# The FFN's opening in a two-layer diffusion backbone: the first token quarter split earlier, four blocks' first products ahead of the sums, the sums' halves laid out by need

## The chip, the cores and the metric

The kernel runs on one core of a Trainium2 chip. The metric is the device time of one execution in microseconds (us); the time of a kernel is the median of its runs. Engines are named as the profile names them: PE (TensorE), PEld (its weight loads), DVE (VectorE), ACT (ScalarE), POOL (GpSimd), SP (SyncE, which only issues DMAs here).

## What is computed

Two layers of a backbone over 512 latent tokens and 256 context tokens of width 1024. Each layer has a mixing sub-layer (three scan mixers side by side and one output projection) and a SwiGLU feed-forward network (FFN) with 2816 hidden channels. Layer 0 computes both token groups through the FFN (768 tokens), layer 1 only the latent ones (512 tokens). What matters here is the end of the mixing sub-layer and the FFN:

```python
mixed_l = jnp.concatenate([gla_l, ssd_l, ret_l], axis=-1) @ w_out[l]
lat = lat + gt1 * rms_norm(mixed_l, norm_mix_post[l])
h_l = modulate(rms_norm(lat, norm_ffn_pre[l]), sh2, sc2)
lat = lat + gt2 * rms_norm(swiglu(h_l, ffn_w13[l], ffn_w2[l]), norm_ffn_post[l])

def swiglu(h, w13, w2):
    gate, up = jnp.split(h @ w13, 2, axis=-1)
    return (jax.nn.silu(gate) * up) @ w2
```

## The kernel before

**Numbers in halves.** Every large matmul is done on pairs: a value x is stored as hi (x cast to a narrower format, by ACT) and lo (x minus hi, by DVE or POOL), and each product is three matmuls, hi·hi, hi·lo and lo·hi. `split` (line 366) does it for a weight tile (`whi` on line 368, `wlo` on line 369), `rsplit` (line 1261) for activations.

**The FFN's first matmul as a 2x2 scheme with seven products.** The activations `whole` (written by `pre_norm` in the output projection stage, one block of 128 tokens after another) are cut into four quarters: b11 and b21 are the lower and upper 512 channels of the first half of the tokens, b12 and b22 those of the second half. For each of 22 blocks of 128 hidden channels (`ffn_up(f)`), the two weight columns are cut into a11, a12, a21, a22, and seven products are taken: a11·b11, a12·b21, s2·t2, s3·t3, s1·t1, a22·t4, s4·b22, where t1 to t4 are sums and differences of the quarters of the activations and s1 to s4 those of the weights. A product (`prod`, its matmuls on line 1289) is 12 matmuls of 384 columns in layer 0 and of 256 columns in layer 1. The weights' sums are made in `load13`: two on POOL (lines 417, 418), two on DVE (lines 419, 420), after the raw weights have landed (DMA on line 405), and are then split. The raw tiles stand in two places that alternate by block: even blocks in pool `wp`, odd blocks in pool `F`.

**The opening.** a11·b11 and a12·b21 need no sums, so for the first NA blocks (3 in layer 0, 4 in layer 1) they are taken ahead (`up_first`, `up_gate`, lines 1295 to 1305), with a weight unit of their own (`w13a`, which holds only a11 and a12). `ffn_up` of these blocks then does the other five products. Before that, per 128 tokens of the first half: the split of b11 (lo on DVE) and of b21 (lo on POOL), the sums t1, t2, t4 (DVE, lines 1275, 1276, 1278) and t3 (POOL, line 1277), the splits of t1 to t4 (lo on DVE) and of b22 (lo on POOL). All four sums' hi halves share one 24 KB buffer of pool `hp`, all lo halves the other; that other buffer is the one that holds `whole`, so no lo half of a sum can be written before the last reader of `whole` is done.

**The stage ahead of it.** The output projection runs over 6 blocks of tokens in layer 0 and 4 in layer 1 (`out_front`, `out_back`): transposes, 96 matmuls of a block (line 497), then for the block before it the norm after the projection (`post_norm`), the residual and the norm ahead of the FFN (`pre_norm`: transposes on line 306, scale and shift into `whole` on lines 312 and 314). Between these, PE also takes the matmuls of the adaptive norm's modulation (`Ada.some`: 48 steps in layer 0 and 32 in layer 1, four matmuls each on lines 203 and 206, with a 512 KB weight load `araw` in a ring of three buffers). Most steps stand ahead of the output stage in the program, the last ten of layer 0 and the last two of layer 1 behind it.

**What sets the order.** The program is written in order; a planner places each instruction on its engine's queue by that order and its own estimate of times, and each engine then works its queue strictly in order. Pools of SBUF are stacks that lie on each other's ground: the pools of the opening, `F`, `FB` and `HR`, are opened when the output stage's pools and the modulation's pool `adp` are closed, and take their place.

Of the kernel before, what the change touches and what calls it, by code (L numbers as in the profile page):

```python
# [11 lines left out]
F32 = mybir.dt.float32  # L12
# [70 lines left out]
def tile_backbone(ctx: ExitStack, tc: tile.TileContext, a: dict, out: bass.AP, dbg=None):  # L83
# [364 lines left out]
    for l in range(NL):  # L448
# [23 lines left out]
        NA = 3 if l + 1 < NL else 4  # L472
# [94 lines left out]
    for l in range(NL):  # L567
# [587 lines left out]
        ada.some(len(ada.todo) - 12)  # L1155
# [9 lines left out]
        whole = pt(hp, "H", [128, 8, tot])  # L1165

# [59 lines left out]
        ada.some(len(ada.todo))  # L1226
        rx.close()
        mx.close()
        ax.close()


        hn = tot // 2
        npos = tot // 128
        n2 = npos // 2
# [13 lines left out]
        fx = ctx.enter_context(ExitStack())  # L1248
        HR = fx.enter_context(pool(f"HR{l}", side="right"))
        FB = fx.enter_context(pool(f"FB{l}", side="right"))  # L1250
        with pool(f"F{l}") as F:
            state["F"] = F
            bhi = pt(FB, "bhi", [128, 3, 4, hn], F32R, bufs=1)
            blo = pt(FB, "blo", [128, 3, 4, hn], F32R, bufs=1)
            tm = pt(FB, "tm", [128, 4, 4, hn], bufs=1)
            thi = pt(hp, "H", [128, 4, 4, hn], F32R)
            tlo = pt(hp, "H", [128, 4, 4, hn], F32R)
            rhs = {"b11": (bhi[:, 0], blo[:, 0]), "b21": (bhi[:, 1], blo[:, 1]), "b22": (bhi[:, 2], blo[:, 2])}
            rhs |= {f"t{q + 1}": (thi[:, q], tlo[:, q]) for q in range(4)}

            def rsplit(nm, src, cs, eng):
                hi, lo = (x[:, :, cs] for x in rhs[nm])
                S.copy(hi, src)  # L1263
                eng.tensor_tensor(lo, src, hi.bitcast(F32), ALU.subtract)  # L1264

            for i in range(n2):
                cs = slice(128 * i, 128 * i + 128)
                rsplit("b11", whole[:, 0:4, cs], cs, V)
                rsplit("b21", whole[:, 4:8, cs], cs, G)
            for i in range(n2):  # L1270
# [3 lines left out]
                t1, t2, t3, t4 = (tm[:, q, :, cs] for q in range(4))  # L1274
# [4 lines left out]
            for i in range(n2):  # L1279
                cs = slice(128 * i, 128 * i + 128)  # L1280
                for nm, q in (("t2", 1), ("t3", 2), ("t1", 0), ("t4", 3)):
                    rsplit(nm, tm[:, q, :, cs], cs, V)
                rsplit("b22", whole[:, 4:8, hn + 128 * i:hn + 128 * i + 128], cs, G)

            def prod(ps, un, wn, rn, first):
                w, r = un[wn], rhs[rn]
                for k in range(4):
                    for p, (x, y) in enumerate(((0, 0), (0, 1), (1, 0))):
                        PE.matmul(ps[:, :hn], w[x][:, k], r[y][:, k], start=first and k == 0 and p == 0,  # L1289
                                  stop=k == 3 and p == 2, skip_group_check=True)  # L1290

            def ut(tag, bufs=2):
                return pt(F, tag, [128, hn], bufs=bufs)

            def up_first(pa, un):
                prod(pa, un, "a11", "b11", True)
                uu = ut("uu", NA + 1)
                S.copy(uu, pa[:, :hn])
                return uu

            def up_gate(pa, un):
                prod(pa, un, "a12", "b21", False)
                g1 = ut("g1", NA + 1)
                S.activation(g1, pa[:, :hn], AF.Silu)
                return g1

            def ffn_up(f, begun):
# [3 lines left out]
                if begun is None:  # L1311
                    pa = mm()
                    uu = up_first(pa, un)
# [12 lines left out]
                if begun is None:  # L1326
                    g1 = up_gate(pa, un)
# [10 lines left out]
            begun = {}  # L1338
            for f in range(NA):
                un = get(u["w13a"][f])  # L1340
                ps = [mm(), px()][f % 2]
                uu = up_first(ps, un)
                begun[f] = uu, up_gate(ps, un)
            for f in range(NF):
                ffn_up(f, begun.get(f))
                if f == 9:
                    he = pt(FB, "tm", [128, 2, 2, 2, tot], F32R, bufs=1)
                    for i in range(2):
                        hr = pt(HR, "hr", [128, 2, tot], bufs=2)
                        hid_load(hr, 2 * i)  # L1350
                        early[2 * i] = hid_split(hr, he[:, i, 0], he[:, i, 1])
# [24 lines left out]
        fx.close()  # L1376
        with pool(f"D{l}") as Dp:
# [80 lines left out]
```

## Time and profile before

| | |
|---|---|
| runs (us) | 1885.75 median of 3; 1882.15 to 1890.06 |
| the profiled execution's own time | 1890.13 us |
| its span | 1888.3 us |
| mean granted PE clock | 0.953 of full |
| PE busy | 1757.6 us, 93% of the span |
| PEld, DVE, ACT, POOL busy | 84%, 62%, 42%, 32% of the span |

The busy share is a mean over stages. The page's 40 slices show where PE is not full: the slices of the two FFN openings (about 540 to 580 us in layer 0, 1510 to 1543 us in layer 1) stand out, with a lower busy share and a lower granted clock. Where a row of a timeline ends in a bracket, it tells how long the engine sat idle before it and what ended that.

### The profile page before, as it was taken

What the parts mean: (1) busy time and instruction counts of PE and PEld (TensorE: products, weight loads), DVE (VectorE), ACT (ScalarE), POOL (GpSimd) and SP (SyncE); (2) the same over time, 40 slices, a digit from 0 to 9 for tenths busy, and PEclk for the clock granted to TensorE, in tenths of its full rate; (3) what the DMA queues carried; (4) which work ended last, traced back from release to release, by engine and by line L of the source; (5) the groups of instructions that cost most, each with busy time, mean ns of one, the idle gap of its engine ahead of it and who ended that gap; (6) DMA issues with size and microseconds to landing.
All of it is one profiled execution on the core that took longest, in us unless ns stands there. A gap on an engine that the chain in (4) does not pass through costs nothing. (4 is left out here: it accounts for less than half of the span.)

```text
span 1888.3 us, 30443 instructions
## 1 busy us (share of the span) xinstructions
PE 1757.6 (93%) x11899; PEld 1589.9 (84%) x11899; DVE 1162.9 (62%) x1963; ACT 793.5 (42%) x1439; POOL 601.6 (32%) x588
## 2 busy tenths in 40 slices
PE   5899999999969999999899989999978879999998
PEld 4678889997868999999788777889966869999886
DVE  4476687746466655654333437678855478888445
ACT  3545443235563333333333465534423554444343
POOL 1102533204233532332322240063302146555322
PEclk9899999999979999999999989999967989999999
DMA  8434464127633433332645374355415245444663
GB/s 273 141 123 137 141 201 161 53 76 259 227 107 116 128 104 93 93 102 81 240 139 202 113 237 136 101 157 165 151 51 170 85 119 149 135 140 129 241 208 132
DMA packets 238189, 274.63 MB, mean 145 GB/s; under 512 B 14041, under 2 KB 181437, under 8 KB 238045
## 3 DMA queue, kind: packets, MB, share of 16 engines
q1 hardware_dynamic: 236832, 270.77, 44.7%
q8 instruction: 93, 1.52, 0.3%
q10 hardware_dynamic: 1212, 1.91, 0.3%
q14 instruction: 52, 0.42, 0.1%
HBM read 233.72 MB, written 38.93 MB: 144 GB/s over the span
## 5 line engine op out<-in xcount | busy, mean ns | idle before, releaser
L369 DVE TENSOR_TENSOR wlo<-raw,whi 128x1024 fp32r<-128x1024 f32 (+2 forms) x192 | 264.8, 1385 | 164.2 <-ACT whi L368 164.1
L1289 PE MATMUL px<-H,whi 128*128 128x384 f32 (+1 forms) x1408 | 308.5, 311 | 8.2 <-ACT whi L368 8.0
L368 ACT CAST whi<-raw 128x1024 fp32r<-128x1024 f32 (+2 forms) x192 | 194.0, 1018 | 233.6 <-PE px L1289 90.0
L497 PE MATMUL mm<-whi,H 128*128 128x256 f32 x1376 | 272.8, 293 | 11.7 <-ACT stg L611 6.4
L1289 PEld LDWEIGHTS px<-H,whi 128*128 128x128 f32 x1408 | 235.6, 190 | 10.5 <-ACT whi L368 10.1
L497 PEld LDWEIGHTS mm<-whi,H 128*128 128x128 f32 x1376 | 223.8, 196 | 22.5 <-ACT stg L611 8.2
L1289 PE MATMUL px<-H,wlo 128*128 128x384 f32 (+1 forms) x704 | 212.1, 311 | 1.8 <-DVE wlo L369 1.8
L497 PE MATMUL mm<-wlo,H 128*128 128x256 f32 x688 | 201.0, 292 | 0.0
L497 PE MATMUL mm<-H,whi 128*128 128x256 f32 (+2 forms) x720 | 177.9, 339 | 8.8 <-DVE H L559 4.0
L497 PEld LDWEIGHTS mm<-H,whi 128*128 128x128 f32 (+1 forms) x720 | 123.1, 190 | 28.8 <-DVE H L559 4.5
L368 ACT CAST whi<-S 128x1024 fp32r<-128x1024 f32 x88 | 73.6, 836 | 160.0 <-DVE S L419 87.6
L497 PEld LDWEIGHTS mm<-wlo,H 128*128 128x128 f32 x688 | 135.5, 197 | 1.4
L1289 PEld LDWEIGHTS px<-H,wlo 128*128 128x128 f32 x704 | 131.6, 190 | 3.0 <-DVE wlo L369 3.0
L1244 POOL TENSOR_TENSOR hidlo<-hr,hidhi 128x768 fp32r<-128x768 f32 (+1 forms) x40 | 70.5, 1763 | 188.9 <-ACT hidhi L1243 176.5
L1330 POOL TENSOR_TENSOR hf<-hf,g 128x384 f32<-128x384 f32 (+1 forms) x44 | 56.7, 1288 | 218.8 <-issue 141.3
L497 PE MATMUL px<-whi,H 128*128 128x256 f32 x640 | 119.7, 286 | 6.3 <-DVE H L1203 3.7
L497 PE MATMUL mm<-H,wlo 128*128 128x256 f32 (+2 forms) x360 | 120.7, 335 | 0.0
L369 DVE TENSOR_TENSOR wlo<-S,whi 128x1024 fp32r<-128x1024 f32 x88 | 92.2, 1048 | 41.4 <-ACT whi L368 41.2
L1289 PE MATMUL mm<-blo,whi 128*128 128x384 f32 (+1 forms) x328 | 103.3, 315 | 9.0 <-DVE blo L1264 9.0
L497 PEld LDWEIGHTS px<-whi,H 128*128 128x128 f32 x640 | 99.5, 190 | 13.6 <-DVE H L1203 5.1
L1365 PE MATMUL px<-wlo,hidhi 128*128 128x512 f32 x276 | 108.7, 394 | 0.0
L1289 PE MATMUL mm<-bhi,whi 128*128 128x384 f32 (+1 forms) x328 | 103.6, 316 | 4.6 <-ACT bhi L1263 3.3
(317 smaller groups left out, 4117.1 us busy)
## 6 DMA issues: line engine op xcount, KB each, us to landing
raw<-ffn_w_dram SPq DMA_DIRECT2D x99, 512.0 KB
araw<-ada_w_dram SPq DMA_DIRECT2D x96, 512.0 KB
raw<-w_in_dram SPq DMA_DIRECT2D x26, 1024.0 KB
raw<-ffn_w_dram SPq DMA_DIRECT2D x20, 1024.0 KB
hr<-hd SPq DMA_DIRECT2D x22, 768.0 KB
hr<-hd SPq DMA_DIRECT2D x22, 512.0 KB
Rt<-gd SPq DMA_DIRECT2D x40, 256.0 KB
hd<-hf SPq DMA_DIRECT2D x22, 384.0 KB
```

Of the source, the lines that this page charges most:

```text
L368: S.copy(hi, src)
L369: lo_engine.tensor_tensor(lo, src, hi.bitcast(F32), ALU.subtract)
L497: PE.matmul(ps, x(k), y(k), start=(k == 0 and p == 0), stop=(k == n - 1 and p == 2))
L1244: (G if q else V).tensor_tensor(lo[:, q], hr[:, q], hi[:, q].bitcast(F32), ALU.subtract)
L1289: PE.matmul(ps[:, :hn], w[x][:, k], r[y][:, k], start=first and k == 0 and p == 0, stop=k == 3 and p == 2, skip_group_check=True)
L1330: G.tensor_tensor(h1, h1, g1, ALU.mult)
L1365: PE.matmul(ps, lh[x](k), rh[y](k), start=f + k == 0 and p == 0, stop=f + k == NF - 1 and p == 2, skip_group_check=True)
```

## The change

- In `out_back`, for the first half of the token blocks, b11 is split as soon as its block is normed: hi on ACT, lo on DVE in two pieces. It stands in buffers of pool `adp` (the constants' tile and two of the three `araw` buffers), which stays open until the FFN's first matmul is done. All modulation steps are therefore put ahead of the output stage in the program.
- NA is 4 in both layers. The first product of all four blocks comes first, each into its own PSUM bank, which it keeps; then b21 is split, then the second products follow; then the sums.
- Each 128 tokens' sums are split as they are made, in the order t1, t2, split t2, t3, split t3, t4, split b22. t2 and t3 (hi and lo) share the first 24 KB buffer, which is free when the output stage's matmuls end; t1 and t4 stay unsplit in `FB` and are split last, in one piece each, into the buffer of `whole`.
- All sums and lo halves of activations are on DVE; POOL has none of them any more.
- The pools: `uu` and `g1` (results of the first and second product) move from `F` to `FB`, `FB` opens before `HR`, the buffer `hr` for early hidden loads is single instead of double, `F` lies above `adp` instead of on its ground.

```diff
-        NA = 3 if l + 1 < NL else 4
+        NA = 4
...
-        ada.some(len(ada.todo) - 12)
+        ada.some(len(ada.todo))
...
+        b11h = pt(adp, "cst2", [128, 4, hn], F32R, bufs=1)
+        b11l = [pt(adp, "araw", [128, 2, hn], F32R, bufs=NRAW) for _ in range(2)]
...
             pre_norm(nps, l, 2, tb, x, whole, pos)
+            if pos < n2:
+                cs = slice(128 * pos, 128 * pos + 128)
+                S.copy(b11h[:, :, cs], whole[:, 0:4, cs])
+                for q in range(2):
+                    ks = slice(2 * q, 2 * q + 2)
+                    V.tensor_tensor(b11l[q][:, :, cs], whole[:, ks, cs], b11h[:, ks, cs].bitcast(F32), ALU.subtract)
...
-        ada.some(len(ada.todo))
         rx.close()
         mx.close()
-        ax.close()
...
+        FB = fx.enter_context(pool(f"FB{l}", 2, side="right"))
         HR = fx.enter_context(pool(f"HR{l}", side="right"))
-        FB = fx.enter_context(pool(f"FB{l}", side="right"))
...
+            uus = [ut("uu", NA + 1) for _ in range(NA)]
+            g1s = [ut("g1", NA + 1) for _ in range(NA)]
+            bh = pt(FB, "bh", [128, 2, 4, hn], F32R, bufs=1)
+            bl = pt(FB, "bl", [128, 2, 4, hn], F32R, bufs=1)
+            ta = pt(hp, "H", [128, 4, 4, hn], F32R)
+            t14, t23 = (pt(FB, "tm", [128, 2, 4, hn]) for _ in range(2))
...
+            def combine(i):
                 cs = slice(128 * i, 128 * i + 128)
...
                 V.tensor_tensor(t1, b12, b11, ALU.subtract)
                 V.tensor_tensor(t2, b22, t1, ALU.subtract)
-                G.tensor_tensor(t3, b22, b12, ALU.subtract)
+                rsplit("t2", t2, cs)
+                V.tensor_tensor(t3, b22, b12, ALU.subtract)
+                rsplit("t3", t3, cs)
                 V.tensor_tensor(t4, b21, t2, ALU.subtract)
+                rsplit("b22", b22, cs)
...
-            begun = {}
+            begun = []
             for f in range(NA):
-                un = get(u["w13a"][f])
-                ps = [mm(), px()][f % 2]
-                uu = up_first(ps, un)
-                begun[f] = uu, up_gate(ps, un)
+                un = get(u["w13a"][f], 0)
+                ps = mm() if f < 2 else px()
+                up_first(ps, un, uus[f])
+                begun.append((ps, un))
+            for i in range(n2):
+                cs = slice(128 * i, 128 * i + 128)
+                rsplit("b21", whole[:, 4:8, cs], cs)
+            for f, (ps, un) in enumerate(begun):
+                up_gate(ps, un, g1s[f])
+            for i in range(n2):
+                combine(i)
+            tb_ = pt(hp, "H", [128, 4, 4, hn], F32R)
...
+            for q, nm in enumerate(("t1", "t4")):
+                rsplit(nm, t14[:, q], allsl)
...
                     for i in range(2):
-                        hr = pt(HR, "hr", [128, 2, tot], bufs=2)
+                        he = pt(FB, "tm", [128, 2, 2, tot], F32R)
+                        hr = pt(HR, "hr", [128, 2, tot], bufs=1)
...
         fx.close()
+        ax.close()
```

## Rows read from the trace of the kernel before

**Rows 1.** The page: span, and busy time of each engine.
```profile
span 1888.3 us, 30443 instructions
PE 1757.6 (93%) x11899; PEld 1589.9 (84%) x11899; DVE 1162.9 (62%) x1963; ACT 793.5 (42%) x1439; POOL 601.6 (32%) x588
```
**Rows 2.** Windows, both openings: length, busy (count) of PE PEld DVE ACT POOL, clock, DMA.
```profile
537.00:577.00 40.00, 20.77 (x111) 18.83 (x110) 30.36 (x47) 23.92 (x45) 22.38 (x13) 0.73 0.28 79
1510.00:1543.20 33.20, 21.37 (x111) 18.69 (x109) 24.45 (x35) 20.20 (x40) 12.23 (x10) 0.74 0.40 111
```
**Rows 3.** Timeline of PE, layer 0: start, duration, instruction, idle before it.
```profile
545.08 1.97 PE L306 MATMUL px<-cst,xn 128*128 128x128 f32 x8 [6.01 <-ACT xn L297]
549.77 0.69 PE L1289 MATMUL mm<-bhi,whi 128*128 128x384 f32 x1 [1.87 <-ACT bhi L1263]
557.20 0.69 PE L1289 MATMUL mm<-blo,whi 128*128 128x384 f32 x1 [6.75 <-DVE blo L1264]
571.66 0.34 PE L1289 MATMUL mm<-blo,whi 128*128 128x384 f32 x1
571.84 0.34 PE L1289 MATMUL mm<-bhi,wlo 128*128 128x384 f32 x1
576.78 2.29 PE L1289 MATMUL px<-H,whi 128*128 128x384 f32 x6 [4.60 <-ACT whi L368]
592.73 0.52 PE L1289 MATMUL px<-H,wlo 128*128 128x384 f32 x2
```
**Rows 4.** Timeline of POOL, both layers: the weight sums that wait for their load.
```profile
569.97 3.61 POOL L417 TENSOR_TENSOR S<-raw 128x512 f32<-128x512 f32 x1 [4.86 <-DMA raw<-ffn_w_dram]
...
1538.72 1.27 POOL L417 TENSOR_TENSOR S<-raw 128x512 f32<-128x512 f32 x1 [11.85 <-DMA raw<-ffn_w_dram]
```
**Rows 5.** Timelines of SP, ACT and DVE, layer 0: weight load, first splits.
```profile
547.96 0.38 SPq L405 DMA_DIRECT2D raw<-ffn_w_dram  x1
...
526.69 1.05 ACT L368 CAST whi<-raw 128x1024 fp32r<-128x1024 f32 x1 [0.74 <-PE px L497]
...
547.03 2.17 ACT L1263 CAST bhi<-H 128x512 fp32r<-128x512 f32 x4
...
546.23 0.41 DVE L314 TENSOR_SCALAR H<-px,modc 128x128 f32<-128x128 f32 x1 [3.02 <-PE px L306]
558.36 0.40 DVE L314 TENSOR_SCALAR H<-px,modc 128x128 f32<-128x128 f32 x1
```
**Rows 6.** Groups by line from 537 to 577: count | busy us, mean ns.
```profile
L1264 POOL TENSOR_TENSOR blo<-H,bhi 128x512 fp32r<-128x512 f32 x6 | 10.1, 1705 | 1.9 <-ACT bhi L1263 1.9
L1264 DVE TENSOR_TENSOR H<-tm,H 128x512 fp32r<-128x512 f32 x12 | 7.3, 683 | 1.2 <-POOL blo L1264 1.2
L1264 DVE TENSOR_TENSOR blo<-H,bhi 128x512 fp32r<-128x512 f32 x3 | 4.8, 1610 | 0.0
L369 DVE TENSOR_TENSOR wlo<-raw,whi 128x1024 fp32r<-128x1024 f32 x2 | 2.3, 1210 | 0.0
```
**Rows 7.** Timelines, layer 1: PE, SP and ACT around the weights' loads.
```profile
1550.99 1.23 PE L1289 MATMUL px<-H,whi 128*128 128x256 f32 x6
...
1516.63 0.42 SPq L405 DMA_DIRECT2D raw<-ffn_w_dram  x1
1528.59 0.38 SPq L405 DMA_DIRECT2D raw<-ffn_w_dram  x1
1532.73 0.99 SPq L405 DMA_DIRECT2D raw<-ffn_w_dram  x2
...
1532.61 1.05 ACT L368 CAST whi<-raw 128x1024 fp32r<-128x1024 f32 x1 [1.08 <-DMA raw<-ffn_w_dram]
```
**Rows 8.** Timeline of PE: modulation steps at a block's boundary in layer 0.
```profile
508.04 0.38 PE L203 MATMUL pa<-araw,sil 128*32 128x256 f32 x1
...
508.26 0.38 PE L203 MATMUL pa<-araw,sil 128*32 128x256 f32 x1
...
509.93 0.50 PE L497 MATMUL px<-whi,H 128*128 128x256 f32 x2 [0.59 <-DVE H L1203]
```

More of the change, by code (lines that the diff above doesn't have):

```diff
@@ L1248, in tile_backbone, with ut, rsplit @@
         fx = ctx.enter_context(ExitStack())
+        FB = fx.enter_context(pool(f"FB{l}", 2, side="right"))
         HR = fx.enter_context(pool(f"HR{l}", side="right"))
-        FB = fx.enter_context(pool(f"FB{l}", side="right"))
         with pool(f"F{l}") as F:
             state["F"] = F
[L1253 to L1262, printed above, removed]
-                S.copy(hi, src)
[L1264 to L1270, printed above, removed]
+            def ut(tag, bufs=2):
+                return pt(FB if tag in ("uu", "g1") else F, tag, [128, hn], bufs=bufs)
+            uus = [ut("uu", NA + 1) for _ in range(NA)]
[4 more added lines that the diff above has]
+            t14, t23 = (pt(FB, "tm", [128, 2, 4, hn]) for _ in range(2))
+            hip = {"b21": bh[:, 0], "b22": bh[:, 1], "t2": ta[:, 0], "t3": ta[:, 2]}
+            lop = {"b21": bl[:, 0], "b22": bl[:, 1], "t2": ta[:, 1], "t3": ta[:, 3]}
+            rhs = {}
+            rhs["b11"] = (lambda k: b11h[:, k]), (lambda k: b11l[k // 2][:, k % 2])
+            def rsplit(nm, src, cs):
+                hi, lo = hip[nm][:, :, cs], lop[nm][:, :, cs]
+                S.copy(hi, src)
+                V.tensor_tensor(lo, src, hi.bitcast(F32), ALU.subtract)
+                rhs[nm] = tuple((lambda k, t=t: t[:, k]) for t in (hip[nm], lop[nm]))
+            def combine(i):
                 cs = slice(128 * i, 128 * i + 128)
@@ L1273, in tile_backbone @@
                 b11, b12, b21, b22 = whole[:, 0:4, cs], whole[:, 0:4, c2], whole[:, 4:8, cs], whole[:, 4:8, c2]
-                t1, t2, t3, t4 = (tm[:, q, :, cs] for q in range(4))
+                t1, t4, t2, t3 = t14[:, 0, :, cs], t14[:, 1, :, cs], t23[:, 0, :, cs], t23[:, 1, :, cs]
                 V.tensor_tensor(t1, b12, b11, ALU.subtract)
                 V.tensor_tensor(t2, b22, t1, ALU.subtract)
-                G.tensor_tensor(t3, b22, b12, ALU.subtract)
+                rsplit("t2", t2, cs)
+                V.tensor_tensor(t3, b22, b12, ALU.subtract)
+                rsplit("t3", t3, cs)
                 V.tensor_tensor(t4, b21, t2, ALU.subtract)
[L1279 to L1283, printed above, removed]
+                rsplit("b22", b22, cs)
             def prod(ps, un, wn, rn, first):
@@ L1288, in prod, with up_first, up_gate @@
                     for p, (x, y) in enumerate(((0, 0), (0, 1), (1, 0))):
-                        PE.matmul(ps[:, :hn], w[x][:, k], r[y][:, k], start=first and k == 0 and p == 0,
+                        PE.matmul(ps[:, :hn], w[x][:, k], r[y](k), start=first and k == 0 and p == 0,
                                   stop=k == 3 and p == 2, skip_group_check=True)
-            def ut(tag, bufs=2):
-                return pt(F, tag, [128, hn], bufs=bufs)
-            def up_first(pa, un):
+            def up_first(pa, un, uu):
                 prod(pa, un, "a11", "b11", True)
-                uu = ut("uu", NA + 1)
                 S.copy(uu, pa[:, :hn])
-                return uu
-            def up_gate(pa, un):
+            def up_gate(pa, un, g1):
                 prod(pa, un, "a12", "b21", False)
-                g1 = ut("g1", NA + 1)
                 S.activation(g1, pa[:, :hn], AF.Silu)
-                return g1
             def ffn_up(f, begun):
@@ L1312, in ffn_up @@
                     pa = mm()
-                    uu = up_first(pa, un)
+                    uu, g1 = ut("uu", NA + 1), ut("g1", NA + 1)
+                    up_first(pa, un, uu)
                 else:
```

14 lines of the change are left out of this document (8 added, 6 removed).

## The prediction

> **What bounds the kernel now.** I read the page's busy shares first [rows 1]: PE is busy 93% of the span, so over the kernel as a whole only PE's work and PE's gaps count. Then I asked where the gaps are, with the windows view. In the two FFN openings PE is busy 20.8 of 40.0 us and 21.4 of 33.2 us, at a granted clock of 0.73 and 0.74 [rows 2]; the reader is to see that these 73 us are the only places where the change can win, and that the other engines are not full there either (DVE 30.4 of 40.0 us and 24.5 of 33.2). So no engine bounds an opening; a chain of waits does.
>
> PE's timeline of layer 0 names the waits [rows 3]. It idles 6.01 us until the last block is normed, 1.87 until the first hi half of b11, 6.75 until the last lo half of b11, and 4.60 until the weights' sums are cast: 19.2 us. The row at 557.20 tells the odd part: b11 is the *first half* of the tokens, ready long before, and PE waits for its lo half after the last block. The reason is the queue. ACT starts the splits only at 547.03, behind the last block's norm [rows 5]. The fourth wait goes back to a load: POOL, 4.86 us idle, gets block 0's raw weights at 569.97 [rows 4], because the buffer they land in is freed by the third `w13a` unit, whose splits stand behind the second one's, whose load was issued at 547.96 [rows 5].
>
> In layer 1 the same row of POOL shows 11.85 us of waiting until 1538.72 [rows 4]; the load was issued at 1532.73 [rows 7].
>
> **How the times relate.** The profiled execution took 1890.13 us, 1.8 more than its span, and lies 4.4 above the median of the runs, 1885.75. I make the sum against 1890.13 and take the difference to the median.
>
> **Part 1, b11 split in the output stage.** It adds one cast on ACT and two subtractions on DVE per block of tokens, three blocks in layer 0 and two in layer 1. They lie beside the block's 96 matmuls; DVE's operation of this size costs 0.68 us alone [rows 6], so at most 1.4 us per block. If that cover were gone, PE would pay it at each block boundary, where it already waits 0.59 us for DVE [rows 8]: 5 x 1.4 = 7 us as an upper bound, taken as 0, because the planner puts these behind the next block's transposes. What it buys: the first product needs nothing of the last block, so it can run in the 6.01 us hole. Only one can: block 0's weights were cast at 526.69, the others wait for the load that was issued at 547.96 [rows 5].
>
> **Part 2, that load.** Before, its buffer lay on the modulation's, and the last modulation step ended in the opening. Now it lies on the mixers' `vvg`, which is done long before; SP, in order, reaches it after the last block's residual is stored, at about 542. A 512 KB load lands 4.0 us after issue (1528.59 to 1532.61 [rows 7]). So the second unit is in at 546 to 547 instead of 552, and the third, whose raw tile waits in its own buffer, follows it. Block 0's full weights then land about 10 us earlier, near 560: the load is no longer what is late.
>
> **Part 3, DVE, which becomes late.** All of POOL's lo halves and t3 go to DVE. From 546.2, when DVE gets the first piece of the last block [rows 5], it owes in layer 0, up to the first weights' halves that product s2·t2 needs:
> - four pieces of the last block at 0.41 us: 1.6
> - three lo halves of b21, nine of t2, t3 and b22, twelve sums: 24 at 0.68: 16.3
> - lo of t1 and t4, 1536 columns each; 0.68 for 512 and 1.21 for 1024 columns make about 1.74: 3.5
> - three lo halves of `w13a` units and two of block 0: 5 at 1.21: 6.1
> - two weight sums at 0.68: 1.4
>
> Together 28.9 us of durations. Operations overlap at their ends: the row of twelve has 7.3 us of busy time, 0.61 each, against a mean of 0.683 [rows 6]. By that ratio it is 26 us, and DVE is through at 572. PE has meanwhile done all eight first and second products (8 x 2.1 us, 12 matmuls at the 0.18 us between the rows of 571.66 and 571.84 [rows 3], from about 549 on except the first), and has waited some us, so its clock is at the lower of its two levels again, as after the 4.60 us wait: there six matmuls take 2.29 us where six at 0.18 take 1.1. I put that at 2.6 us, both before and after. Five products at 2.1 us then end between 582 (two of them taken while DVE finishes) and 585. Before, at 592.73 PE had done the six early products and, from 576.78, what fits into 16 us less the 2.6 lost to the clock: 74 matmuls at 0.18. That makes 146, ten short of the 156 that thirteen products are, so it was level at 594 to 595. The gain is 9 to 12 us; I take 10. Afterwards PE runs without gaps in both.
>
> The third part hangs on what POOL's company costs DVE. The same subtraction takes 0.683 us in the run of twelve and 1.610 us while POOL runs its own, which take 1.705 [rows 6]. The Trainium skill, page "SBUF — State Buffer", section "Who interferes with whom", says that a DVE instruction with two SBUF inputs and a GpSimd instruction that reads SBUF take a shared port as an exclusive lock, one blocking the other for its whole length. By that rule the nine operations that leave POOL cost DVE nothing net; if the two engines ran side by side instead, DVE would be through 9 x 0.61 = 5.5 us later than before for the same work. [...] The rows above side with the first.
>
> **Part 4, layer 1.** Four blocks already stood ahead there, so PE's work is the same. The F load is issued at 1516.63, right behind the last residual's store [rows 7], and lands at 1520.6. Unit 2 and unit 3 are split by about 1524 (a cast and a lo half each, ACT and DVE side by side, 1.2 us apart), where before the third unit's buffer came free at 1532.7. In front of block 0's full weights SP still has the fourth unit's load, so I count 1527 to 1528 for them instead of 1532.73, and 5 us less on the row 1538.72. DVE's sums for two times 128 tokens are through before. The end of block 0, 1550.99 [rows 7], moves by 4 to 5 us. After it the stage goes at the pace of the weights, which moves along with it. I take 4.5.
>
> **Part 5, the modulation moved up.** Ten steps in layer 0 and two in layer 1, with their 512 KB loads on SP, now stand ahead of the output stage. Before, PE took them at the block boundaries, in time in which it had to wait anyway: a step is 0.22 us (508.04 to 508.26), and behind them PE still idles 0.59 us [rows 8]. Placed amid the matmuls instead, they cost PE 12 x 0.22 = 2.6 us; if the planner leaves them at the boundaries, nothing. The lower bound excludes a gain in the output stage; what leaves the opening (the last modulation's transposes and DVE additions) is already out of the list above. I take 2.
>
> **Part 6, the rest.** The extra 512 KB for layer 0's fourth early block lies in a stretch with a DMA share of 0.28 [rows 2]: nothing. The single `hr` holds SP until the first early load is split; SP then stands before weight loads, at most one load, 4 us per layer, more likely nothing. For a queue order that fits the chip badly I take 1.5: in layer 0 the last block's final piece, ready at 547, was done at 558.36 [rows 5], because the planner had expected it late.
>
> **Sum.** 10 + 4.5 - 2 - 1.5 = 11 us: 1879 for an execution like the profiled one, 1875 against the median. About 0.5% is what a measurement of this kernel can tell from no change.
>
> **The rivals.**
> - *DVE takes the place of POOL's load* (given back). If DVE's operations keep their longer times (POOL's sums of weights stay, and the hi halves from ACT arrive one by one), its 26 us are 30, layer 0 gains 6 and layer 1, where its own list grows by the same operations, 2: with parts 5 and 6 that is 4 to 5, about 1881. For it: DVE is the engine with the most work in both windows [rows 2]. Against: without POOL's lo halves the company is gone.
> - *The holes close entirely.* If the planner lets sums of the first token blocks run before 546, DVE is through at 566 or earlier, PE never stands and keeps its clock: 10 + 6 + 2.6 in layer 0 and the clock's part in layer 1, about 22 net, 1864. Against: splits of layer 0 started at 547.03 although their memory and sources were mostly free.
> - *Slower: PE waits for modulation loads in the output stage.* Steps amid matmuls stand in PE's in-order queue, and all matmuls wait behind one whose load is late. Some thirteen steps run after the stage's second block, in four to five groups of up to three loads; a load takes 4.0 us and three that share the queues more. If each group is 5 us late, 25 us are lost, 10 more than the 14.5 of the openings: 1896. It decides from 3 us per group. Against: before, PE idles at the boundary for DVE, never for such a load [rows 8].
> - *It doesn't do what it says*: weights of units 2 and 3 still behind the last block, one early product only. That is already in the forecast; it is why I don't count the 19.2 us as won.
>
> **How the numbers follow.** Forecast 0.50, 1869 to 1881, likeliest 1875. Given back 0.27, 1878 to 1886. Holes closed 0.12, 1858 to 1868. Slower 0.11, 1890 to 1900. The range 1860 to 1889 leaves out the slow rival and the best of the third. Faster by over 0.5% (below 1876.3): 0.12, two thirds of the forecast, 0.05 of the given back: 0.50. Slower by over 0.5% (above 1895.2): 0.09. Within: 0.41.
>
> **What would show it.** Right: the first product with b11's early halves (named by their buffers, `cst2` and `araw`) lies between the last output matmul and the last transposes; the F load is issued near 542; eight early products end before 567; s2·t2 starts near 570 to 572 behind DVE, not behind a load. Wrong: POOL's first sum still waits for its load in layer 0 (part 2); PE idles for `araw` between 490 and 530 (part 5); DVE idles while PE waits for it (part 3, order instead of load).

## The result, and the profile after

| | before | after |
|---|---|---|
| median of the runs (us) | 1887.82 (1882.15 to 1890.06) | 1919.44 (1910.64 to 1924.1) |
| ratio to before | | 1.0173, 95% interval 1.0151 to 1.0195 |
| profiled execution (us), its span | 1890.13, 1888.3 | 1910.64, 1908.9 |
| mean granted PE clock | 0.953 | 0.948 |

The change makes the kernel 31.6 us slower (six runs of each; three of before were on record with the prediction, median 1885.75). The forecast was 1875, in a range of 1860 to 1889; the time lies above it, and above the slow rival's 1890 to 1900. The profiled execution of after is its fastest, 8.8 us under its median, so its span shows 20.6 of the 31.6 us.

The page of after: the span, and each engine's busy time. Against [rows 1] PE has lost 4.9 us of busy time and the span is longer, so time was added in which PE stands.

```profile
span 1908.9 us, 30428 instructions
PE 1752.7 (92%) x11899; PEld 1578.2 (83%) x11899; DVE 1163.4 (61%) x1977; ACT 795.0 (42%) x1433; POOL 574.6 (30%) x573
```

Where it stands is seen in the windows of after from 440 to 490 us (length, busy time and count of PE, PEld, DVE, ACT, POOL, granted clock, DMA share, GB/s), the stretch in which the kernel before runs the first half of layer 0's output projection:

```profile
440.00:450.00 10.00, 2.82 (x29) 1.36 (x26) 7.61 (x16) 7.21 (x16) 0.70 (x2) 0.86 1.05 399
450.00:460.00 10.00, 1.93 (x16) 0.59 (x16) 2.74 (x4) 2.59 (x4) 8.87 (x6) 0.50 0.97 329
460.00:470.00 10.00, 7.86 (x48) 3.94 (x48) 3.79 (x8) 4.07 (x9) 3.46 (x3) 0.50 0.94 317
470.00:480.00 10.00, 5.17 (x46) 1.19 (x42) 3.32 (x8) 4.10 (x9) 3.62 (x3) 0.67 0.93 333
480.00:490.00 10.00, 5.54 (x44) 1.00 (x40) 1.70 (x4) 1.60 (x4) 2.19 (x2) 0.50 0.64 209
```

PE is busy 23.3 of 50 us, for long at the lower of its two clock levels (granted 0.50), while the DMA engines are near full until 480. PE's timeline of after tells what it does there (start, duration, instruction, idle time before it and what ended that):

```profile
456.31 0.63 PE L203 MATMUL pa<-araw,sil 128*32 128x256 f32 x1 [11.48 <-DVE araw L217]
...
475.84 0.61 PE L203 MATMUL pa<-araw,sil 128*32 128x256 f32 x1 [2.02 <-DMA araw<-ada_w_dram]
...
488.89 0.64 PE L203 MATMUL pa<-araw,sil 128*32 128x256 f32 x1 [1.28 <-DMA araw<-ada_w_dram]
...
490.47 0.69 PE L226 MATMUL px<-cst,araw 128*128 128x128 f32 x2 [0.49 <-ACT araw L221]
490.81 0.56 PE L497 MATMUL px<-whi,H 128*128 128x256 f32 x1
```

It takes modulation steps, most of them as their loads land, and transposes (line 1205) of the blocks that are to be projected, but not one output matmul until 490.81. The longest wait, 11.48 us, ends with DVE's addition (line 217) into a buffer of the loads' ring; the other waits of line 203 shown here end with a landed load. The first output matmul (line 497) comes directly behind the transposes that end the last modulation (line 226). In the kernel before the same matmul starts 42.3 us earlier, and modulation steps follow among the output matmuls:

```profile
448.52 0.39 PE L497 MATMUL px<-whi,H 128*128 128x256 f32 x1
```

The openings did what they were meant to, in part. The windows of after from the end of the last output matmul to the start of the 156th matmul of the products (13 products of 12 matmuls; in after the eight early ones and block 0's five), layer 0 and layer 1, and then the same stretches of before:

```profile
572.20:619.80 47.60, 33.32 (x171) 30.45 (x170) 36.97 (x56) 27.03 (x44) 6.58 (x7) 0.89 0.35 100
1530.50:1571.20 40.70, 26.67 (x171) 24.47 (x170) 28.23 (x45) 21.96 (x39) 8.38 (x7) 0.79 0.42 117
```

```profile
537.20:594.10 56.90, 37.67 (x191) 35.73 (x190) 40.70 (x61) 28.26 (x50) 28.93 (x18) 0.76 0.33 93
1509.90:1550.90 41.00, 28.94 (x172) 26.05 (x171) 30.30 (x43) 22.96 (x43) 15.40 (x13) 0.79 0.42 116
```

9.3 us are gained in layer 0 and 0.3 in layer 1. With the marks of PE's timelines (us) the span can be added up; the last two columns are kernels of the study below:

| PE's timeline | before | after | 2nd experiment | 9th experiment |
|---|---|---|---|---|
| layer 0: first output matmul | 448.5 | 490.8 | 444.8 | 443.1 |
| last output matmul ends | 537.2 | 572.2 | 537.5 | 535.1 |
| 156th product matmul | 594.1 | 619.8 | 585.2 | 578.7 |
| last product ends | 889.5 | 917.8 | 883.1 | 874.6 |
| layer 1: first output matmul | 1451.0 | 1477.4 | 1446.1 | 1432.1 |
| last output matmul ends | 1509.9 | 1530.5 | 1499.7 | 1489.4 |
| 156th product matmul | 1550.9 | 1571.2 | 1540.7 | 1522.4 |
| last product ends | 1760.4 | 1781.0 | 1751.5 | 1731.5 |
| span | 1888.3 | 1908.9 | 1879.4 | 1859.2 |

After against before: +42.3 until layer 0's output stage starts, -7.3 in that stage (it has no modulation in it any more), -9.3 in the opening, +2.6 in the later blocks, -1.9 up to layer 1's output stage, -5.8 in that stage, -0.3 in its opening, and +0.3 until the last product: 20.6, the whole difference of the spans.

The rest of the openings' waits, in after, on PE in layer 0 and on POOL in both layers, answer to [rows 3] and [rows 4]:

```profile
580.06 1.83 PE L306 MATMUL px<-cst,xn 128*128 128x128 f32 x8 [4.91 <-ACT xn L297]
583.96 0.69 PE L1296 MATMUL mm<-bh,whi 128*128 128x384 f32 x1 [2.07 <-ACT bh L1275]
587.15 0.69 PE L1296 MATMUL mm<-cst,whi 128*128 128x384 f32 x1 [2.51 <-ACT whi L368]
...
605.34 1.76 PE L1296 MATMUL px<-H,whi 128*128 128x384 f32 x6 [2.68 <-ACT whi L368]
```

```profile
600.84 1.29 POOL L417 TENSOR_TENSOR S<-raw 128x512 f32<-128x512 f32 x1 [22.01 <-DVE H L1276]
...
1557.57 1.28 POOL L417 TENSOR_TENSOR S<-raw 128x512 f32<-128x512 f32 x1 [16.75 <-DMA raw<-ffn_w_dram]
```

One product runs before the last block's transposes, then b21's halves, the second unit's weights and block 0's weights are waited for. In layer 0 POOL's row names DVE's last split, which ended just then, and not the load; block 0's second load was issued 6.7 us earlier, at 594.12, and in the second experiment's kernel it is again 6.7 us from this issue to the sum, with the load named. POOL's first sum starts 28.7 us after the last output matmul in layer 0 and 27.1 in layer 1, against 32.8 and 28.8 before: late as ever.

### The profile page after: what moved, and what is told of

It is laid out like the page before. It is cut to its first block, busy times and chain, and to the rows that moved or that the text cites. A ratio compares the mean times of both kernels' runs of the same rounds, so it can differ in the third digit from the quotient of the medians.

```text
span 1908.9 us, 30428 instructions
## 1 busy us (share of the span) xinstructions
PE 1752.7 (92%) x11899; PEld 1578.2 (83%) x11899; DVE 1163.4 (61%) x1977; ACT 795.0 (42%) x1433; POOL 574.6 (30%) x573
## 5 line engine op out<-in xcount | busy, mean ns | idle before, releaser
L1379 PE MATMUL px<-whi,hidhi 128*128 128x512 f32 x276 | 107.3, 393 | 0.0
L1379 PE MATMUL px<-whi,hidlo 128*128 128x512 f32 x276 | 105.9, 389 | 0.0
```

What stands on the lines that cost most here:

```text
L1379: PE.matmul(ps, lh[x](k), rh[y](k), start=f + k == 0 and p == 0, stop=f + k == NF - 1 and p == 2, skip_group_check=True)
```

## The experiments

Below, "the second kernel" is the kernel of the second experiment, and so on. Each experiment's time stands beside the kernel before, run again in the same set: 1887.84 us for experiments 1 to 4, 1887.24 for 5 to 8, 1885.16 for 9 to 12; the ratios are against it.

Theory A: the 42.3 us come from PSUM, the memory that PE's results go to. `px` is the tag of five banks of it. `ada_finish` takes a px bank for its transposes on line 224, and the planner gives out the buffers of one tag in program order. With all modulations written ahead of the output stage, the stage's accumulators (`po = [px(), px()]`) can't be had before the last modulation has its bank, and that one waits for every modulation load. Theory B: the loads and steps stand ahead in the queues of SP and PE (the slow rival of the prediction, at a higher price). Theory C: the new opening is what loses.

**1. The kernel before, modulation moved up, nothing else.**

```diff
-        ada.some(len(ada.todo) - 12)
+        ada.some(len(ada.todo))
```

> The kernel before with one edit: all modulation steps stand ahead of the output projection stage in the program, as in the changed kernel; nothing of the opening is touched. Theory A (the stage's accumulators px are given out in program order, behind the px that the last modulation's transposes take, and those wait for every modulation load): the first output matmul of layer 0 starts near 490 us instead of 448.5, the stage itself is some 7 us shorter, layer 1's stage 5 us shorter, so 25 to 36 us over the kernel before, ratio 1.013 to 1.019. Theory C (the changed opening is what loses, through DVE's longer list): within 3 us of the kernel before.

Measured: 1929.5 us against 1887.84, ratio 1.0219, interval 1.018 to 1.0258. This line alone loses 41.7 us, more than the whole change and more than the 25 to 36 that A had allowed: the stage starts at 494.7, not near 490. C falls: the opening, unchanged here, takes 56.9 us as in before. PE's timeline of this kernel has the same pair of rows as after:

```profile
494.34 0.69 PE L226 MATMUL px<-cst,araw 128*128 128x128 f32 x2 [0.49 <-ACT araw L221]
...
494.68 0.56 PE L497 MATMUL px<-whi,H 128*128 128x256 f32 x1
```

**2. The changed kernel, the transposes in the modulation's own bank.**

```diff
-        pst = px()
+        pst = psa.tile([128, 512], F32, tag="pa", name="pa")
```

> The changed kernel with one edit: the transposes at a modulation's end take the PSUM bank of the modulation's own accumulator (pa) instead of a px bank. All modulation loads still stand ahead of the output stage in the program. Theory A (px given out in program order): the first output matmul of layer 0 starts within 448 to 456 us, modulation steps lie among the output matmuls, and the 9 us that layer 0's opening gained remain: 1868 to 1884, ratio 0.989 to 0.998. Theory B (the loads themselves, ahead in the queues of SP and PE, hold the matmuls up): the start stays above 480 and the time above 1905, ratio above 1.01.

Measured: 1883.31 us, ratio 0.9963, interval 0.9937 to 0.9989. All loads stand where the change put them, yet the output stage starts on time, and the last modulation's transposes come 28.7 us after it, in PE's timeline:

```profile
444.85 0.39 PE L497 MATMUL px<-whi,H 128*128 128x256 f32 x1
...
473.51 0.38 PE L226 MATMUL pa<-cst,araw 128*128 128x128 f32 x2
```

A stands, B falls. One bank name is worth 36.1 us (1919.44 against 1883.31). What remains of the change is a gain of 4.5 us, less than the 0.5% that the prediction set as its limit.

**3. The kernel before with both edits.**

> The kernel before with both edits: all modulation steps ahead of the output stage in the program, and the transposes at a modulation's end in the bank pa. Opening as before. Theory A: first output matmul 448 to 456 us, time within 4 us of the kernel before or up to 6 us under it (no modulation work is left at the last block's boundary). Theory B: as the first of these, 25 to 36 us over the kernel before.

Measured: 1888.77 us, ratio 1.0012, interval 0.9992 to 1.0031. Moving the modulation costs nothing measurable once the bank is another one; against the first experiment the bank is worth 40.7 us.

**4. The kernel before, two steps more ahead of the stage.**

```diff
-        ada.some(len(ada.todo) - 12)
+        ada.some(len(ada.todo) - 8)
```

> The kernel before with eight instead of ten modulation steps left behind layer 0's output stage: two more steps ahead, with which one more modulation (and its px for the transposes) is finished ahead of the stage. In the changed kernel the transposes of that modulation stand at 473.4 us. Theory A: a jump for two steps, the first output matmul at 470 to 477 us, time 12 to 25 us over the kernel before, ratio 1.006 to 1.013. Theory B (time goes with the number of loads moved ahead): two tenths of what moving all ten costs, 5 to 8 us at most, start below 458.

Measured: 1913.06 us, ratio 1.0144, interval 1.0108 to 1.0179: 25.2 us for two steps of PE's work, just above the 12 to 25 (ratio 1.006 to 1.013) that A allowed and far from B's 5 to 8. The second of the two finishes a modulation, and the stage starts behind its transposes:

```profile
473.49 0.69 PE L226 MATMUL px<-cst,araw 128*128 128x128 f32 x2 [0.49 <-ACT araw L221]
...
473.83 0.56 PE L497 MATMUL px<-whi,H 128*128 128x256 f32 x1
```

The price goes by which modulation's bank stands ahead of the stage, not by the number of loads. With 1 to 4, A is shown.

The next question is why the openings gained 9.6 us where 14.5 were forecast, and what bounds them now. In the second kernel POOL's timeline still has the load of block 0's weights as the last wait in both layers, and in layer 0 ACT casts the second and third early unit (one row, x2) only at 551.41, though SP issues their loads at 542.52 and 530.09. Their lo halves follow on DVE, and only behind these does SP issue the next loads (the fourth unit's at 557.92, block 0's two at 559.06 and 559.48). POOL's rows, then layer 0's rows of SP, ACT and DVE:

```profile
566.14 1.30 POOL L417 TENSOR_TENSOR S<-raw 128x512 f32<-128x512 f32 x1 [22.00 <-DMA raw<-ffn_w_dram]
...
1527.50 1.29 POOL L417 TENSOR_TENSOR S<-raw 128x512 f32<-128x512 f32 x1 [17.47 <-DMA raw<-ffn_w_dram]
```

```profile
530.09 0.38 SPq L405 DMA_DIRECT2D raw<-ffn_w_dram  x1
...
551.41 2.00 ACT L368 CAST whi<-raw 128x1024 fp32r<-128x1024 f32 x2
...
556.68 2.35 DVE L369 TENSOR_TENSOR wlo<-raw,whi 128x1024 fp32r<-128x1024 f32 x2
...
557.92 2.13 SPq L405 DMA_DIRECT2D raw<-ffn_w_dram  x3
...
561.98 1.05 ACT L368 CAST whi<-raw 128x1024 fp32r<-128x1024 f32 x1 [1.49 <-DMA raw<-ffn_w_dram]
```

**5. The second kernel, early units in pairs in one raw tile.** A unit that holds only a11 and a12 fills half a raw tile; the third and fourth now use the other half of the first's and second's.

```diff
-        raw = wtile(F if f % 2 else wp, "raw", [128, 4, 512])
+        gate = srcs["gate_only"]
+        if gate and f >= 2:
+            raw = state["pair", f % 2]
+        else:
+            raw = wtile(F if f % 2 else wp, "raw", [128, 4, 512])
+        if gate and f < 2:
+            state["pair", f] = raw
+        h = 0 if gate and f >= 2 else 2
...
```

(what is left out makes the early load and its split use the half `h`)

> The changed kernel with the modulation's transposes in the bank pa (the second kernel of this study, 1883.3 us), and one more edit: the third and fourth early unit land in the free half of the raw tile of the first and second, so that the four early loads wait for no split of one another. Theory L (layer 0's and layer 1's openings still wait for block 0's raw weights, 566.14 and 1527.50 us in that kernel, because their load stands behind early loads that wait for splits, and these stand on ACT and DVE behind the last block's norm): POOL's first sum moves up by 8 to 14 us in layer 0 and 6 to 12 in layer 1; the openings gain 3 to 5 and 5 to 8 us; 1871 to 1876, ratio 0.990 to 0.994 of the kernel before. Rival D (DVE's own list is through at 573 us and decides): POOL's sum moves up but the product s2 t2 stays within 2 us; total gain 0 to 4 us, 1879 to 1883.

Measured: 1875.66 us, ratio 0.9938, interval 0.9916 to 0.9959. That is inside theory L's range, but not by L's way: the interval overlaps the second kernel's, and by the traces the openings gain 1.0 us together. Layer 1's takes 38.6 us instead of 41.0, where L wanted 5 to 8, and POOL's first sum there comes at 1525.32, 2.2 us earlier, where L wanted 6 to 12; layer 0's takes 49.1 instead of 47.7. In layer 0 POOL's sum did not move, though SP issues the third unit's load now with the first's, at 467.71: its cast comes 85 us later, with the second's. ACT's row and POOL's of both layers:

```profile
552.53 1.99 ACT L368 CAST whi<-raw 128x1024 fp32r<-128x1024 f32 x2
...
566.26 2.20 POOL L424 TENSOR_TENSOR S<-raw 128x512 f32<-128x512 f32 x1 [21.10 <-DMA raw<-ffn_w_dram]
...
1525.32 1.28 POOL L424 TENSOR_TENSOR S<-raw 128x512 f32<-128x512 f32 x1 [16.04 <-DMA raw<-ffn_w_dram]
```

**6. The second kernel, three early blocks in layer 0.**

> The second kernel of this study (modulation's transposes in pa) with three early blocks instead of four in layer 0; layer 1 unchanged. Theory L: block 0's raw weights land one load of about 4 us earlier (562 instead of 566), but PE has two products less to do ahead: within 3 us of 1883. Rival D (DVE decides): block 0's products start as before at 570, and the two products that are not done ahead are done behind it: 2 to 5 us slower, 1885 to 1888.

Measured: 1883.74 us, ratio 0.9981, interval 0.9957 to 1.0004; not to be told from the second kernel. By the trace layer 0's opening takes 53.4 us, 5.7 more, and POOL's sum starts 30.1 us after the last output matmul, no earlier than with four. So the fourth load is not what delayed block 0's, against L, and by the trace the fourth early block is 5.7 of the 9.3 us that layer 0 gained; the medians do not show it.

**7. The fifth kernel, b21's and b22's lo halves and t3 back on POOL.**

```diff
-                V.tensor_tensor(t3, b22, b12, ALU.subtract)
+                G.tensor_tensor(t3, b22, b12, ALU.subtract)
```

(and `rsplit` of b21 and b22 with G for the lo half)

> The first kernel of this job (raw tiles in pairs), and the lo halves of b21 and b22 and the sum t3 back on POOL as in the kernel before: 9 operations of DVE less in layer 0, 6 in layer 1. If DVE and POOL take turns at a shared port (the reading on which part 3 of the prediction rested), DVE's remaining operations get longer by as much: within 2 us of the first kernel of this job, or slower. If they run side by side, DVE's list is 5.5 us shorter in layer 0 and 3.6 in layer 1, and where DVE decides the openings gain that: 4 to 9 us faster than the first kernel of this job. Rows to look at: the mean of the 128x512 subtractions on DVE, 0.68 us alone.

Measured: 1880.37 us, ratio 0.9961, interval 0.9941 to 0.9981: 4.7 us slower than the fifth kernel by the medians; the intervals overlap, and by the traces the difference lies outside the openings, which take 49.0 and 39.1 us against 49.1 and 38.6. The windows of both openings, this kernel's and then the fifth's:

```profile
542.60:591.60 49.00, 35.19 (x173) 32.66 (x172) 39.54 (x47) 27.00 (x44) 22.30 (x16) 0.83 0.36 97
1502.70:1541.80 39.10, 25.56 (x172) 23.57 (x171) 29.32 (x39) 21.85 (x39) 16.35 (x13) 0.78 0.46 122
...
538.50:587.60 49.10, 36.00 (x172) 33.62 (x170) 36.68 (x56) 26.97 (x44) 8.17 (x7) 0.79 0.36 97
1498.90:1537.50 38.60, 25.95 (x173) 23.94 (x172) 28.15 (x45) 21.51 (x39) 8.41 (x7) 0.78 0.46 123
```

With nine operations fewer in layer 0 and six in layer 1, DVE is busy 2.9 and 1.2 us longer. So the move gains nothing, where running side by side was expected to gain 4 to 9 us; that it loses is not shown. The groups by line, layer 0's opening, tell why (busy us, mean ns, idle before). DVE's sum t4 in the seventh kernel:

```profile
L1296 DVE TENSOR_TENSOR tm<-H,tm 128x512 f32<-128x512 f32 x3 | 4.2, 1416 | 0.0
```

in the fifth kernel, with the lo halves of b21 and b22 that it has on DVE:

```profile
L1283 DVE TENSOR_TENSOR bl<-H,bh 128x512 fp32r<-128x512 f32 x6 | 4.0, 687 | 0.0
L1296 DVE TENSOR_TENSOR tm<-H,tm 128x512 f32<-128x512 f32 x3 | 2.1, 693 | 0.0
```

and POOL's lo halves in the seventh:

```profile
L1283 POOL TENSOR_TENSOR bl<-H,bh 128x512 fp32r<-128x512 f32 x6 | 10.3, 1746 | 1.4 <-ACT bh L1282 1.4
```

The same DVE operation takes twice as long beside POOL, and POOL takes 1.75 us for what DVE does in 0.69. Work moved to POOL takes DVE's time all the same.

**8. The second kernel, the last modulation steps behind the third block's output matmuls.** There PE waits 4.66 us at 479.13 for `gt`.

```diff
+            if pos == n2 - 1:
+                ada.some(len(ada.todo))
...
```

(the call ahead of the stage leaves them again, as in the kernel before; b11's splits then follow the first half's last norm, since their buffers are the modulation's)

> The second kernel of this study (modulation's transposes in pa), with the last ten modulation steps of layer 0 and the last two of layer 1 behind the third (layer 1: second) block's output matmuls instead of ahead of the stage, and b11's splits of the first half's blocks all after the last of these blocks' norm, since their buffers are the modulation's. Theory: in that kernel PE waits 4.66 us at 474.5 for gt, whose load stands on SP behind modulation loads, and then runs some us at the lower clock; that goes, 3 to 7 us faster: 1876 to 1880. Rival (the hole belongs to the gate's chain on ACT and DVE, not to the loads): within 2 us of 1883.

Measured: 1877.91 us, ratio 0.9951, interval 0.9935 to 0.9967, which overlaps that of the second kernel. The wait for `gt` is gone from PE's timeline, and another is there instead:

```profile
477.98 0.40 PE L203 MATMUL pa<-araw,sil 128*32 128x256 f32 x1 [2.95 <-DMA araw<-ada_w_dram]
```

The stage takes 92.8 us as against 92.6. The median falls where the theory wanted it, but inconclusively, and the trace shows no gain where it was expected.

**9. The fifth kernel, early units in the order 0, 2, 1, 3.**

```diff
-        u["w13a"] = [add13(f, True, False) for f in range(NA)]
+        u["w13a"] = {f: add13(f, True, False) for f in (0, 2, 1, 3)}
...
-            for f in range(NA):
+            for n, f in enumerate((0, 2, 1, 3)):
...
```

> The raw-tiles-in-pairs kernel (1875.7 us), with one more edit: the early units are taken in the order 0, 2, 1, 3. In the pairs kernel the third unit's raw data was loaded early (SP issues only two early loads after the last residual's store, at 543.55), yet it was cast only at 552.5 and POOL's first sum came no earlier in layer 0 (566.26 against 566.14). Theory T (whi buffers, too, are given out in program order: the third unit's cast stands behind the second's, whose raw tile waits for pool F): with the order turned, units 0 and 2 are split inside the output stage, two first products run in PE's hole before the last block's transposes, POOL's first sum comes at 550 to 557 in layer 0; 2 to 5 us there and 2 to 4 in layer 1, 1868 to 1873, ratio 0.989 to 0.993. Rival D (DVE's list, through at 573, decides): POOL's sum comes early but s2 t2 starts within 2 us of 571.70; 1873 to 1876.

Measured: 1864.45 us, ratio 0.9895, interval 0.9859 to 0.9932: 20.7 us under the kernel before, and 3.6 us under the low end of what was expected. Theory T holds in this: units 0 and 2, whose raw tile is free early, no longer stand behind unit 1, whose tile waits for pool F. That it is the `whi` buffers that made them stand, and not their place in the queues, is argued from the first four experiments; no run here gave the units other `whi` buffers in the old order. POOL's first sums:

```profile
541.68 1.26 POOL L424 TENSOR_TENSOR S<-raw 128x512 f32<-128x512 f32 x1
...
1498.53 1.35 POOL L424 TENSOR_TENSOR S<-raw 128x512 f32<-128x512 f32 x1
```

They come 6.6 and 9.1 us after the last output matmul, instead of 28.7 and 27.8 in the second kernel. The windows of both openings:

```profile
535.10:578.70 43.60, 34.48 (x172) 31.85 (x171) 35.30 (x54) 25.44 (x42) 7.18 (x6) 0.84 0.33 91
1489.40:1522.40 33.00, 24.46 (x171) 22.99 (x170) 28.25 (x45) 21.24 (x38) 7.51 (x7) 0.79 0.45 120
```

The first product of sums starts at 567.21, 32.1 us after the last output matmul, against 33.2 in the fifth kernel. So the start in layer 0 hardly moved, as rival D had said, but not because DVE decides it: PE arrives there without a wait. In the fifth kernel it had waited 0.77 us for a cast, waited 2.44 for DVE again, and ran on at the lower clock (granted 0.50 from 576 to 580). The ninth kernel's row, then the fifth's:

```profile
567.21 0.69 PE L1303 MATMUL px<-H,whi 128*128 128x384 f32 x3
...
571.70 1.56 PE L1303 MATMUL px<-H,whi 128*128 128x384 f32 x6 [0.77 <-ACT whi L368]
575.69 0.69 PE L1303 MATMUL px<-H,wlo 128*128 128x384 f32 x1 [2.44 <-DVE wlo L369]
```

**10. The ninth kernel with the eighth's spreading.**

> The kernel above this one (order 0, 2, 1, 3) with the last modulation steps behind the third (layer 1: second) block's output matmuls and b11's splits together after these blocks' norms. If the spreading is worth what its own run showed against its base (ratio 0.9951 against 0.9963), 1 to 4 us faster than the kernel above; if that was noise, within 1 us. The version meant to be the fastest: 1866 to 1873.

Measured: 1867.66 us, ratio 0.9911, interval 0.9876 to 0.9945. It is 3.2 us over the ninth by the medians, with intervals that overlap: the 1 to 4 us that the spreading might have won are not seen.

**11. The ninth kernel, b11 split after the output stage.** The program lines of b11's split are moved behind the stage; the buffers stay in pool `adp`.

> The first kernel of this job (order 0, 2, 1, 3) with one part of the change undone: b11 is not split block by block in the output stage but after it, before the first products, as in the kernel before; its buffers stay. If the early halves of b11 are what lets first products run in PE's hole (part 1 of the prediction): no product before the last block's transposes, two products of 2.1 us each later, and DVE's list longer by six pieces of 0.41 us: 3 to 6 us slower in the two layers together. Rival: the hole is filled by nothing that counts, because a later wait takes it back: within 2 us.

Measured: 1862.2 us, ratio 0.9897, interval 0.9851 to 0.9944: no difference. ACT's timeline shows why, first here (where the stage starts at 448.1), then in the ninth kernel (443.1):

```profile
489.85 0.62 ACT L1274 CAST cst<-H 128x512 fp32r<-128x512 f32 x1
```

```profile
484.93 0.62 ACT L1232 CAST cst<-H 128x512 fp32r<-128x512 f32 x1
```

Both are 41.8 us into the stage. The planner splits b11 as soon as its block is normed, on either side of the stage's lines. What then made the kernel before split it late is, by elimination, the ground of its buffers (pool `FB`, which opens behind the stage); no run tried that by itself. The expectation missed.

**12. The kernel before with only the pairs and the order of 5 and 9.**

> The kernel before with only the loads' edit: early units in pairs in one raw tile and in the order 0, 2, 1 (layer 1: 0, 2, 1, 3). Nothing else of the change. Theory L (block 0's raw weights end last in both openings, 569.97 and 1538.72 us in the kernel before): POOL's first sum moves up by 5 us or more in both layers; layer 1 gains 3 to 6, layer 0 2 to 5; 1878 to 1883. Rival: in the kernel before, b11's last lo half at 557.2 and the splits of the sums stand in front, and the openings gain under 2 us together: 1885 to 1888.

Measured: 1879.63 us, ratio 0.9971, interval 0.995 to 0.9992. By the trace the openings take 49.9 and 35.3 us, 12.7 less than before together, more than expected; 6.0 us are lost between layer 0's last product and layer 1's first output matmul, where nothing was edited (PE waits 8.3 us for modulation loads there, 3.7 in before); why is not shown. POOL's sums come at 539.94 and 1518.13, and in layer 0 it is b11's lo half that PE waits for:

```profile
550.89 0.69 PE L1296 MATMUL mm<-blo,whi 128*128 128x384 f32 x1 [6.44 <-DVE blo L1271]
```

The wait of [rows 3] at 557.20 is what the change's buffers take away, and the loads' order is what the change lacked. With both, and the modulation's own bank, the ninth kernel is 15.2 us faster than this one, in the same set and with intervals apart (0.9859 to 0.9932 against 0.995 to 0.9992), 8.6 us of it in the openings: the new opening is a gain once nothing stands in its way.

## Why the prediction was wrong, point by point

- **Part 5 is the step that failed.** It priced the moved modulation by PE's time, 0.22 us a step, with 2.6 us as the upper bound. (A step is two such rows, 160 rows of line 203 for 80 steps, so even that is 5.3.) The first experiment measures 41.7 us, and in after the start of layer 0's output stage is 42.3 us late. The step counted the moved instructions and their DMAs on SP, but not the buffer that a moved block takes ahead of its new neighbours: two modulations' px banks, ahead of the stage's accumulators; the first of the two alone costs 25.2 us (fourth experiment). The remark that PE had never idled for such a load [rows 8] was true of an order in which no accumulator stood behind one.
- **The slow rival had the place right, the mechanism wrong and the size too small.** It let steps amid the matmuls hold PE's queue, at 5 us a group. There were no steps amid the matmuls; the whole stage stood behind them. So its sign, PE idle for `araw` between 490 and 530, did not appear: in after PE idles for `araw` before 490, ahead of the stage. B, its general form, fell in the second and fourth experiment.
- **Part 3, layer 0: right in size.** Forecast 10, measured 9.3 (the same in the second experiment). The sums' first product starts at 570.65 there, forecast 570 to 572, but it waits for weights cast late, not for DVE. Right sum, in part by luck.
- **Part 3's premise on POOL and DVE: right.** The seventh experiment is the direct measurement: 693 ns alone, 1416 beside POOL. It agrees with the Trainium skill, page "SBUF — State Buffer", section "Who interferes with whom" (one engine's access locks the other out). The Trainium skill's page "Perfetto Trace Analysis", section "Optimizing Scalar/DVE Operations", says that a saturated DVE's work may be given to GPSIMD, and adds that it might not help, because the two share a port. It does not help here: the openings are as long with the work on POOL as on DVE (88.1 us together against 87.7).
- **Part 2 failed in its conclusion.** The F load is issued 5.0 us after the last output matmul, as forecast (542 against 537). "The load is no longer what is late" is wrong: block 0's weights come at 566 in the second experiment, not near 560. The third unit does follow the second, as forecast, but the second comes late: its load, issued at 542.52, is cast only at 551.41, behind casts of activations on ACT, and the lo halves come on DVE only at 556.68, so that block 0's loads are issued at 559.06 and 559.48. The third unit, whose load was issued 12.4 us before the second's, stands behind it all that time. POOL's first sum waiting for its load was the prediction's own sign for this. With the order turned POOL's first sum comes at 541.7 instead of 566 (ninth experiment).
- **Part 4 is mis-sized for the same reason.** Forecast 4.5, measured 0.3. With pairs and the turned order layer 1's opening gains 8.0 (41.0 to 33.0).
- **Part 1: the mechanism was read wrongly at the outset.** "The reason is the queue", the prediction said of the splits that start at 547.03 [rows 5]. The eleventh experiment shows that it is not the place of the lines: on `adp` the split runs early even when it is written late. What remains is the ground of the buffer. One early product, as forecast.
- **Part 6** was 1.5; in layer 0 the later blocks lose 2.6. The single `hr` was not tried alone, so whether it is the cause stays open.

The two failures are one: in parts 2 and 5 a step was priced by when its inputs are ready, and what stands ahead of it in program order was left out. For part 5 it is shown that this acts through the order in which a tag's buffers are given out; for part 2 that is argued.

## What to carry to other kernels

Before a block of code is moved in a program whose planner hands out buffers by tag in program order, list the tags that it allocates, and ask which allocation behind it then waits for the slowest input ahead of it; here a bank of its own was all it needed. Where several users of equal buffers stand in one order and the memory of one comes free late, let the users whose memory is free go first. And where the line stands does not decide an early start (eleventh experiment); look at where its buffer lies.

## What the runs showed of the hardware

POOL beside DVE: six lo halves and three sums on POOL took 14.6 us (10.3 and 4.3) for what DVE does in 6.1 (4.0 and 2.1), and lengthened DVE's other 128x512 two-input operations in layer 0's opening by up to 723 ns each (seventh against fifth kernel), while DVE's `TENSOR_SCALAR` from PSUM (line 314) stayed at 407 to 408 ns. Modulation loads in a row came 1.9 us apart (PE's eight steps from 475.84 to 488.89 in after), about half of the 4.0 us from issue to landing that the prediction had for one load of the same size: what a queue of loads delivers is not read from the time of one.
